# Chunk inverses of a recurrent mixer: block products of 64 for both heads in place of block-diagonal products of 128 for each

## The chip, the cores and the metric

One core of a Trainium2 chip runs the whole program. The metric is device time in microseconds of one execution; the time before is the median of three timed runs. TensorE (PE) multiplies matrices into PSUM, VectorE (DVE) and ScalarE (ACT) work on tiles in SBUF and PSUM, GpSimd (POOL) does a little, and SyncE (SP) issues nearly all loads.

## What is computed

The program is a small network of two blocks on 512 tokens of width 1024. In the first block's first layer two recurrent mixers stand side by side, and the change touches one of them, `rwkv7_group`. It has 8 heads of width 64. With the sequence cut into chunks, each chunk solves a triangular system and then passes a state on:

```python
A_ab = pair(a_dec, b_inv, strict)
A_ak = pair(a_dec, k_inv, strict)
rhs = jnp.concatenate([a_dec, jnp.einsum('bhnls,bhnsv->bhnlv', A_ak, v)], axis=-1)
sol = lax.linalg.triangular_solve(jnp.eye(L, dtype=F32) - A_ab, rhs,
                                  left_side=True, lower=True, unit_diagonal=True)
```

`pair` is a masked product of two chunks' rows. The mixers are followed by an output projection, cross-attention, a gated feed-forward, a second layer with other mixers, and a second block with retention, differential attention and a mixture of 32 experts. The outcome is one tensor of 512 x 1024.

## The kernel before

Every wide projection is done by `dense` (line 407): a weight tile is loaded into `raw` by SP, split into a high and a low part (`whi` by ACT at L383, `wlo` by DVE at L384), and 24 matmuls of 512 columns add up in a PSUM tile `acc`. All matmuls go through the helper `mm` (L348), so that the names of their operands tell them apart: `pp<-Q,XP` writes the PSUM tile `pp` from the tiles `Q` and `XP`.

The mixer works with chunks of 64 tokens. A tile of 128 x 512 holds four pairs of chunks: the pair's 128 tokens on the partitions and, side by side, four blocks of 128 columns. `rwkv_front` (the first half) makes the projections and the decayed vectors of two heads; `rwkv_back` (L773) makes the chunk inverses, the outputs and the state of two heads. There are four passes of two heads each. `merge` weaves a pass of `rwkv_back` with the next pass's `rwkv_front`, by the weights 45 and 27, or, in the fourth pass, with the keys and values of the memory (`mem_kv`). It calls in turn the part that is least far on for its weight, by the numbers that each `yield` gives. This sets priorities; the scheduler then fixes the order on each engine, and each engine runs its order strictly.

In `rwkv_back`, `pair(e, ...)` (L788) makes the products for head `e`: 64 rows of the array (that head's 64 components), 128 x 128 results, of which only the two diagonal blocks of 64 x 64 mean anything, as a chunk has nothing to do with its neighbour. `Am` holds A for one head. `X` and `P` are the inverse and its transpose, started as the identity with the first level copied in by a mask (L811 to L818). Then five levels double the size of the blocks that are solved (L843 on). At each level, for each head:

```python
pq = prod(Am[e], P[e])
TT(t4(Q[e]), t4(pq), b4(self.c("levt", l)), op=OP.mult)
...
pp = prod(X[e], Q[e])
if l < 5:
    px = prod(Q[e], X[e])
TT(P[e], pp, P[e], op=OP.add)
```

`prod` (L799) is four fp32 matmuls of 128 x 128 by 128 columns, one for each pair of chunks. So Q needs P; P and X need Q; the next level's Q needs P. The head-by-head order gives two such chains. `rest()` supplies the other products of the pass (`aak`, `Arb`, `Ark`, `pv`) between the levels. After the last level `prod(P[e], R[e])` gives Z (`pp<-R,XP`), and the state goes from chunk to chunk (`pT`, `pS`, `pw`, `py`).

Small tiles of 128 x 512 (`Am`, `Q`, `Z` and so on) come from a ring of 23 buffers, `self.f`; PSUM tiles of one bank each from a pool of five, `self.px`.

Three groups of small matmuls elsewhere in the trace are 64 x 64, each in one quadrant of the array (its rows are the partitions of the operands, its columns those of the result). `po<-qd,S` in `gla` alternates the halves `us` of the result, with the rows of one head, into one PSUM tile. `pkv<-vt,ket` in `gla` goes through both chunks of a pair (rows) and both heads (columns), with one PSUM tile for each chunk. `py<-reff,S` in `rwkv_back` has for head 0 the upper rows and the lower half of the result, for head 1 the opposite, with one PSUM tile for each head.

Of the kernel before, what the change touches and what calls it, by code (L numbers as in the profile page):

```python
# [11 lines left out]
I32 = mybir.dt.int32  # L12
AF = mybir.ActivationFunctionType
OP = mybir.AluOpType
# [168 lines left out]
def constants():  # L183
    A = {}
    i = np.arange(128)
    ident = np.eye(128, dtype=np.float32)
    c = i // 64
# [10 lines left out]
    for l in range(6):  # L198
# [3 lines left out]
        lev.append(off.astype(np.float32))  # L202
    A["cm"] = np.ascontiguousarray(np.concatenate(
        [ident, bones, bsw, m_incl, m_incl_sw, m_strict_sw, lev[0]] + [x.T for x in lev], axis=1))
    seg = np.ones((128, 512), np.float32)
    seg[:, ::64] = 0.0
    A["seg64"] = seg
# [74 lines left out]
class Net:  # L282
# [363 lines left out]
    def rwkv_lora(self):  # L646

        nc, A = self.nc, self.A
        self.vz = []
        for j in range(2):  # L650
            t = self.per.tile([128, 4, 192], F32, name=f"vz{j}")
            nc.gpsimd.memset(t[:, :, 64:128], 0.0)
            self.vz.append(t)
        self.wa2, self.wg2, self.lr, self.sgl = self.four("lora")
        self.yb = self.four("y")
        nc.sync.dma_start(self.wa2, A["rw_wa2"])
        nc.sync.dma_start(self.wg2, A["rw_g2"])
        lr = self.shift(self.dense(A["w_ab"], 8, 8, self.x), self.v("mu_lr1"), "lr", self.lr)
        nc.scalar.activation(lr[:64], lr[:64], AF.Tanh)
        yield 5  # L660
        sgl = self.shift(self.dense(A["w_ab"], 9, 8, self.x), self.v("mu_lr2"), "sgl", self.sgl)
        nc.scalar.activation(sgl, sgl, AF.Sigmoid)
        yield 5
# [109 lines left out]
    def rwkv_back(self, p, d, y):  # L773
# [6 lines left out]
        fs = slice(128 * p, 128 * p + 128)  # L780
        adec, binv, kinv, rdec, R, vt, ZV, BKt, sd, v = (
            d[n] for n in ("adec", "binv", "kinv", "rdec", "R", "vt", "ZV", "BKt", "sd", "v"))
        idb = b4(self.ident)
        rr = [slice(64 * e, 64 * e + 64) for e in range(2)]
        hc = [slice(64 - 64 * e, 128 - 64 * e) for e in range(2)]
        tiles = [slice(i * 128, i * 128 + 128) for i in range(4)]
# [9 lines left out]
            TT(t4(t), t4(ps), b4(self.c(mask)), op=OP.mult)  # L796
            return t

        def prod(x, z):  # L799
            ps = self.px("pp")  # L800
            for s in tiles:
                self.mm(ps[:, s], x[:, s], z[:, s])
            return ps


        Am, X, P = [], [], []
        inv = self.four("XP")
        pairs = self.four("Arb")
        for e in range(2):
            x, pt_ = inv[2 * e:2 * e + 2]  # L810
            nc.scalar.copy(t4(x), idb)  # L811
            nc.scalar.copy(t4(pt_), idb)
            ps = pair(e, adec, binv)
            am = self.f("Am")
            nc.scalar.copy(am, ps)
            nc.vector.copy_predicated(t4(x), b4(self.c("lev0").bitcast(I32)), t4(ps))
            ps = pair(e, binv, adec)
            nc.vector.copy_predicated(t4(pt_), b4(self.c("levt").bitcast(I32)), t4(ps))  # L818
            Am.append(am)
            X.append(x)  # L820
            P.append(pt_)
            yield 1.7
        Arb, Ark = [None, None], [None, None]

        def rest():
# [13 lines left out]

        rest = rest()  # L840
        for l in range(1, 6):
            Q = [None, None]
            for e in range(2):  # L843
                pq = prod(Am[e], P[e])
                Q[e] = self.f("Q")
                TT(t4(Q[e]), t4(pq), b4(self.c("levt", l)), op=OP.mult)
                yield 0.9
            for e in range(2):
                pp = prod(X[e], Q[e])
                if l < 5:  # L850
                    px = prod(Q[e], X[e])
                TT(P[e], pp, P[e], op=OP.add)
                if l < 5:
                    TT(X[e], px, X[e], op=OP.add)
                yield 1.7
                next(rest, None)
        for _ in rest:
            yield 0.9
        Z = []
        ZS = self.f("ZS")  # L860
        for e in range(2):
            pz = prod(P[e], R[e])
            z = self.f("Z")
            nc.scalar.copy(t4(ZS)[:, :, rr[e]], t4(pz)[:, :, rr[e]])
            nc.scalar.copy(z, pz)
            for c in range(2):
                nc.scalar.copy(ZV[rr[c], :, c, hc[e]], t4(pz)[rr[c], :, hc[e]])
            Z.append(z)
            yield 0.9
# [1470 lines left out]
def emit(ctx, tc, A, upto="all", dbg=None):  # L2340
    pctx, wctx = ExitStack(), ExitStack()
    N = Net(ctx, pctx, wctx, tc, A)
    ctx.push(pctx)
    ctx.push(wctx)
    nc = tc.nc

    def dump(name, tiles):
        for m, t in enumerate(tiles):
            nc.sync.dma_start(dbg[name][m], t)

    hb = N.four("h") + N.four("h")
    N.pre = []
    for m in range(8):
        N.resid(m, None, "g_mix0", True, hb[m])
        if m in (0, 3):
            N.pre.append(N.split_w2(A["w_gv"], 2 * len(N.pre)))
    nc.sync.dma_start(N.ident_, A["cm"][:, :128])
    y = [None] * 8
    d = [{} for _ in range(4)]

    def head():
        yield from N.rwkv_lora()
        N.memory()
        yield from N.rwkv_front(0, d[0])

    merge((N.gla(y), 95), (head(), 36))
    N.early()
    N.clear(N.zD, N.big("zero"))
    for p in range(4):
        back = (N.rwkv_back(p, d[p], y), 45)  # L2370
        if p < 3:
            merge(back, (N.rwkv_front(p + 1, d[p + 1]), 27))
        else:
            kv = [{}, {}]
            merge(back, (N.mem_kv(0, N.mem_operand(), kv[0]), 48))
    if upto == "rwkv":
        return dump("y", y)
    N.project(A["w_mo"][0], 8, N.operand(y), "g_xa0", first=True)
    if upto == "mix0":
        return dump("y", [N.hD[m] for m in range(8)])  # L2380
    N.xattn(0, kv[0])
    if upto == "xa0":
        return dump("y", [N.hD[m] for m in range(8)])
    ada = N.ada_parts()
    N.ffn(0, "g_mix1", ada[:6])
    if upto == "ffn0":
        return dump("y", [N.hD[m] for m in range(8)])
    y = [None] * 8
    d = [{} for _ in range(4)]

    def two(a):
        yield from N.mlstm_in(a, d[a])
        yield from N.mlstm_in(a + 1, d[a + 1])

    def first():
        yield from N.mlstm_gates()
        yield from two(0)

    merge((N.rglru(y), 51), (first(), 34))
    mo = N.mem_operand()  # L2400
    merge((N.mlstm_head(0, d[0], y), 7), (N.mlstm_head(1, d[1], y), 7), (two(2), 28))
    merge((N.mlstm_head(2, d[2], y), 7), (N.mlstm_head(3, d[3], y), 7), (N.mem_kv(1, mo, kv[1]), 48))
    if upto == "y1":
        return dump("y", y)
    N.project(A["w_mo"][1], 8, N.operand(y), "g_xa1")
    N.xattn(1, kv[1])
    N.ffn(1, None, ada[6:])
    N.norm_pair()
    M = Moe(ctx, N)
    ahead = [M.fetch for _ in range(BIG - 2)]  # L2410
    h2 = N.block2_mix(ahead)
    if upto == "h2":
        return dump("y", h2[0])
    wctx.close()
    N.route(*h2, ahead, M.early)
    pctx.close()
    M.open()
    M.run()
# [17 lines left out]
```

## Time and profile before

| what | value |
|---|---|
| median of three timed runs | 3314.12 us (3313.49 to 3316.09) |
| the profiled execution, its own time | 3308.96 us |
| its span, first instruction to last | 3307.1 us |
| PE busy, share of the span | 3216.8 us, 97% |
| PE weight loads (PEld) | 2564.3 us, 78% |
| DVE busy | 2347.8 us, 71% |
| ACT busy | 1832.9 us, 55% |
| mean granted TensorE clock | 0.987 |

A busy PE means that some matmul is under way; since matmuls are pipelined and overlap, it does not mean that the array is full. An fp32 matmul leaves two records of PE and two of PEld. The timeline merges neighbouring records of one kind: start, time from the first start to the last end, and their number. A row of the lines view gives the count, the busy time, the mean duration of one record, and after the second bar the idle time of the engine ahead of it, with what ended it. The four passes of `rwkv_back` run from 160.9 to 484 us.

### The profile page before, as it was taken

To read this page: it belongs to the slowest core of one execution; us is meant where nothing else is said; L and a number is where in the kernel's file an instruction comes from. 1 tells how busy PE (TensorE), PEld (TensorE's weight loads), DVE (VectorE), ACT (ScalarE), POOL (GpSimd) and SP (SyncE) were. 2 spreads that over 40 slices of the span, in tenths; PEclk is the share of its full clock that TensorE was granted. 3 is DMA by queue.
4 is the path that set the end of the run, shared out by engine and by line. 5 is a ranking of instruction groups with operands and counts; after the bars stand their busy time and mean duration, and the time that the engine had idled before them with its cause. 6 is when DMAs were issued, how large, how long until landed. Compare 5 with 4: busy or idle time off the path is not lost. (4 is left out here: it accounts for less than half of the span.)

```text
span 3307.1 us, 40569 instructions
## 1 busy us (share of the span) xinstructions
PE 3216.8 (97%) x15334; PEld 2564.3 (78%) x15335; DVE 2347.8 (71%) x3023; ACT 1832.9 (55%) x2356; POOL 205.4 (6%) x139
## 2 busy tenths in 40 slices
PE   8999999999999999999999998899999999999997
PEld 6688887777876787777877765688888888788885
DVE  5677765577634665577634354799999999999997
ACT  6643334443425864443434355577777777777774
POOL 1000001100000001100011000100110010111000
PEclk9999999999999999999999999899999999999999
DMA  5201123344333234345334312799999999999994
GB/s 167 79 20 29 43 89 121 122 168 169 90 125 111 75 118 126 126 147 184 90 110 135 128 50 105 275 355 360 366 366 366 353 358 367 359 358 357 369 358 161
DMA packets 152967, 649.61 MB, mean 196 GB/s; under 512 B 21335, under 2 KB 26543, under 8 KB 103228
## 3 DMA queue, kind: packets, MB, share of 16 engines
q1 hardware_dynamic: 143836, 630.86, 52.3%
q0 software_dynamic: 8928, 16.09, 1.9%
q8 instruction: 122, 2.00, 0.2%
q14 instruction: 81, 0.66, 0.1%
HBM read 626.55 MB, written 36.75 MB: 201 GB/s over the span
## 5 line engine op out<-in xcount | busy, mean ns | idle before, releaser
L1990 DVE TENSOR_TENSOR wlo<-w,whi 128x2048 fp32r<-128x2048 f32 x384 | 868.2, 2288 | 81.2 <-ACT whi L1989 76.5
L1989 ACT CAST whi<-w 128x2048 fp32r<-128x2048 f32 x384 | 729.7, 1908 | 295.9 <-PE hid L1981 178.5
L348 PE MATMUL acc<-x,whi 128*128 128x512 f32 (+1 forms) x2656 | 861.9, 404 | 7.2 <-ACT x L420 2.6
L383 ACT CAST whi<-raw 128x512 fp32r<-128x512 f32 (+1 forms) x578 | 352.8, 613 | 727.8 <-PE acc L348 600.6
L384 DVE TENSOR_TENSOR wlo<-raw,whi 128x512 fp32r<-128x512 f32 (+1 forms) x578 | 394.2, 685 | 389.8 <-ACT whi L383 373.5
L348 PEld LDWEIGHTS acc<-x,whi 128*128 128x128 f32 (+1 forms) x2656 | 496.1, 188 | 155.3 <-issue 25.4
L348 PE MATMUL acc<-x,wlo 128*128 128x512 f32 (+1 forms) x1328 | 534.0, 402 | 0.0
L1981 PE MATMUL hid<-whi,xh 128*128 128x512 f32 x1024 | 412.5, 403 | 4.5 <-DVE ln L2084 4.5
L1981 PE MATMUL hid<-whi,xl 128*128 128x512 f32 x1024 | 402.5, 393 | 2.6 <-DVE xl L1990 2.6
L348 PEld LDWEIGHTS acc<-x,wlo 128*128 128x128 f32 (+1 forms) x1328 | 250.0, 188 | 66.1 <-issue 6.3
L1981 PE MATMUL hid<-wlo,xh 128*128 128x512 f32 x1024 | 278.2, 393 | 0.0
L1981 PEld LDWEIGHTS hid<-whi,xh 128*128 128x128 f32 x1024 | 193.8, 189 | 46.2 <-issue 5.5
L1981 PEld LDWEIGHTS hid<-wlo,xh 128*128 128x128 f32 x1024 | 193.5, 189 | 42.7
L1981 PEld LDWEIGHTS hid<-whi,xl 128*128 128x128 f32 x1024 | 194.0, 189 | 41.7 <-DVE xl L1990 3.1
L1981 PE MATMUL y<-whi,ah 128*128 128x512 f32 x512 | 200.8, 392 | 0.7 <-ACT ah L1989 0.7
L1981 PE MATMUL y<-whi,al 128*128 128x512 f32 x512 | 200.3, 391 | 0.9 <-DVE al L1990 0.9
L348 PE MATMUL acc<-act,whi 128*128 128x512 f32 x512 | 162.6, 398 | 0.0
L1981 PE MATMUL y<-wlo,ah 128*128 128x512 f32 x512 | 158.8, 391 | 0.5 <-DVE wlo L1990 0.5
L455 POOL TENSOR_TENSOR sq<-sq,hs 128x512 f32<-128x512 f32 x42 | 56.2, 1339 | 1207.5 <-ACT hs L454 1207.1
L2121 POOL DMA_INDIRECT zD<-ys,sl x30 | 79.0, 2634 | 776.2 <-ACT sel L2043 466.5
L348 PEld LDWEIGHTS acc<-act,whi 128*128 128x128 f32 x512 | 95.2, 188 | 27.0 <-issue 5.1
L1981 PEld LDWEIGHTS y<-whi,ah 128*128 128x128 f32 x512 | 96.1, 188 | 22.6 <-ACT ah L1989 1.1
(651 smaller groups left out, 4653.7 us busy)
## 6 DMA issues: line engine op xcount, KB each, us to landing
w<-in_w_dram SPq DMA_DIRECT2D x384, 1024.0 KB, 8.2
raw<-in_w_up_dram SPq DMA_DIRECT2D x86, 512.0 KB, 3.5
wada<-in_w_ada_dram SPq DMA_DIRECT2D x96, 256.0 KB, 5.0
raw<-in_w_dn_dram SPq DMA_DIRECT2D x32, 512.0 KB, 3.6
h<-hD SPq DMA_DIRECT2D x48, 256.0 KB, 2.8
raw<-in_w_ab_dram SPq DMA_DIRECT2D x22, 512.0 KB, 3.6
hD<-hn SPq DMA_DIRECT2D x40, 256.0 KB, 2.0
raw<-in_w_k_dram SPq DMA_DIRECT2D x16, 512.0 KB, 3.5
```

The costliest lines, as they stand in the source:

```text
L348: self.nc.tensor.matmul(out, l, r, start=start, stop=stop)
L383: nc.scalar.copy(hi[:, :w], raw[:, c:c + w])
L384: nc.vector.tensor_tensor(lo[:, :w], raw[:, c:c + w], hi[:, :w].bitcast(F32), op=OP.subtract)
L455: nc.gpsimd.tensor_tensor(self.sq, self.sq, s, op=OP.add)
L1981: self.nc.tensor.matmul(out, l, r, start=start, stop=stop)
L1989: self.nc.scalar.copy(hi, src)
L1990: self.nc.vector.tensor_tensor(lo, src, hi.bitcast(F32), op=OP.subtract)
L2121: self.nc.gpsimd.indirect_dma_start(out=self.n.zD, out_offset=bass.IndirectOffsetOnAxis(ap=sl[:, 0:1], axis=0), in_=ys, in_offset=None, bo ...
```

## The change

A and the two matrices of the inverse are kept as their diagonal blocks alone: for each chunk a block of 64 x 64, the upper chunk of a pair on partitions 0 to 63, the lower one on 64 to 127. A head then takes 256 columns, and both heads fit in one tile of 128 x 512 (`X`, `P`, `Am`, `Q`). `pair_c` makes the blocks with 16 matmuls of 64 x 64 by 64 columns over the four quadrants of the array, into one PSUM tile for each head. `prod_c` makes one product of a level for both heads with 16 matmuls that alternate between the quadrant of the upper rows and columns and that of the lower ones, into one PSUM tile. The masks of 64 x 64 come as a new constant `cmc`, loaded once into a buffer of the ring. The products with R take 8 matmuls of 128 columns in the same two quadrants for each head. Heads no longer alternate within a level; `next(rest)` is called after Q too, and the weight of `rwkv_back` goes from 45 to 32. Nothing else is touched.

```diff
--- before.py
+++ after.py
@@ -202,6 +202,9 @@
         lev.append(off.astype(np.float32))
     A["cm"] = np.ascontiguousarray(np.concatenate(
         [ident, bones, bsw, m_incl, m_incl_sw, m_strict_sw, lev[0]] + [x.T for x in lev], axis=1))
+
+    A["cmc"] = np.ascontiguousarray(np.concatenate(
+        [np.concatenate([x[:64, :64], x[64:, 64:]]) for x in [ident, lev[0]] + [x.T for x in lev]], axis=1))
     seg = np.ones((128, 512), np.float32)
     seg[:, ::64] = 0.0
     A["seg64"] = seg
@@ -653,6 +656,8 @@
             self.vz.append(t)
         self.wa2, self.wg2, self.lr, self.sgl = self.four("lora")
         self.yb = self.four("y")
+        self.cmc = self.f("cmc")
+        nc.sync.dma_start(self.cmc, A["cmc"])
         nc.sync.dma_start(self.wa2, A["rw_wa2"])
         nc.sync.dma_start(self.wg2, A["rw_g2"])
         lr = self.shift(self.dense(A["w_ab"], 8, 8, self.x), self.v("mu_lr1"), "lr", self.lr)
@@ -780,7 +785,6 @@
         fs = slice(128 * p, 128 * p + 128)
         adec, binv, kinv, rdec, R, vt, ZV, BKt, sd, v = (
             d[n] for n in ("adec", "binv", "kinv", "rdec", "R", "vt", "ZV", "BKt", "sd", "v"))
-        idb = b4(self.ident)
         rr = [slice(64 * e, 64 * e + 64) for e in range(2)]
         hc = [slice(64 - 64 * e, 128 - 64 * e) for e in range(2)]
         tiles = [slice(i * 128, i * 128 + 128) for i in range(4)]
@@ -796,30 +800,44 @@
             TT(t4(t), t4(ps), b4(self.c(mask)), op=OP.mult)
             return t
 
-        def prod(x, z):
+
+
+        t8 = lambda t: t.rearrange("p (i l) -> p i l", l=64)
+        cm = lambda j, n: self.cmc[:, 64 * j:64 * j + 64].unsqueeze(1).to_broadcast([128, n, 64])
+        cols = [slice(j * 64, j * 64 + 64) for j in range(8)]
+        half = [slice(256 * e, 256 * e + 256) for e in range(2)]
+
+        def pair_c(x, z):
+            ps = [self.px("pA") for _ in range(2)]
+            for i in range(4):
+                for c in range(2):
+                    t = slice(128 * i + 64 * c, 128 * i + 64 * c + 64)
+                    for e in range(2):
+                        self.mm(ps[e][rr[c], cols[i]], x[rr[e], t], z[rr[e], t])
+            return [t[:, :256] for t in ps]
+
+        def prod_c(x, z):
             ps = self.px("pp")
-            for s in tiles:
-                self.mm(ps[:, s], x[:, s], z[:, s])
+            for s in cols:
+                for c in range(2):
+                    self.mm(ps[rr[c], s], x[rr[c], s], z[rr[c], s])
             return ps
 
-
-        Am, X, P = [], [], []
         inv = self.four("XP")
+        X, P = inv[:2]
         pairs = self.four("Arb")
+        Am = self.f("Am")
+        for t in (X, P):
+            nc.scalar.copy(t8(t), cm(0, 8))
+        ps = pair_c(adec, binv)
         for e in range(2):
-            x, pt_ = inv[2 * e:2 * e + 2]
-            nc.scalar.copy(t4(x), idb)
-            nc.scalar.copy(t4(pt_), idb)
-            ps = pair(e, adec, binv)
-            am = self.f("Am")
-            nc.scalar.copy(am, ps)
-            nc.vector.copy_predicated(t4(x), b4(self.c("lev0").bitcast(I32)), t4(ps))
-            ps = pair(e, binv, adec)
-            nc.vector.copy_predicated(t4(pt_), b4(self.c("levt").bitcast(I32)), t4(ps))
-            Am.append(am)
-            X.append(x)
-            P.append(pt_)
-            yield 1.7
+            nc.scalar.copy(Am[:, half[e]], ps[e])
+            nc.vector.copy_predicated(t8(X[:, half[e]]), cm(1, 4).bitcast(I32), t8(ps[e]))
+        yield 1.7
+        ps = pair_c(binv, adec)
+        for e in range(2):
+            nc.vector.copy_predicated(t8(P[:, half[e]]), cm(2, 4).bitcast(I32), t8(ps[e]))
+        yield 1.7
         Arb, Ark = [None, None], [None, None]
 
         def rest():
@@ -839,27 +857,28 @@
 
         rest = rest()
         for l in range(1, 6):
-            Q = [None, None]
-            for e in range(2):
-                pq = prod(Am[e], P[e])
-                Q[e] = self.f("Q")
-                TT(t4(Q[e]), t4(pq), b4(self.c("levt", l)), op=OP.mult)
-                yield 0.9
-            for e in range(2):
-                pp = prod(X[e], Q[e])
-                if l < 5:
-                    px = prod(Q[e], X[e])
-                TT(P[e], pp, P[e], op=OP.add)
-                if l < 5:
-                    TT(X[e], px, X[e], op=OP.add)
-                yield 1.7
-                next(rest, None)
+            pq = prod_c(Am, P)
+            Q = self.f("Q")
+            TT(t8(Q), t8(pq), cm(2 + l, 8), op=OP.mult)
+            yield 0.9
+            next(rest, None)
+            pp = prod_c(X, Q)
+            if l < 5:
+                px = prod_c(Q, X)
+            TT(P, pp, P, op=OP.add)
+            if l < 5:
+                TT(X, px, X, op=OP.add)
+            yield 1.7
+            next(rest, None)
         for _ in rest:
             yield 0.9
         Z = []
         ZS = self.f("ZS")
         for e in range(2):
-            pz = prod(P[e], R[e])
+            pz = self.px("pp")
+            for i, s in enumerate(tiles):
+                for c in range(2):
+                    self.mm(pz[rr[c], s], P[rr[c], cols[4 * e + i]], R[e][rr[c], s])
             z = self.f("Z")
             nc.scalar.copy(t4(ZS)[:, :, rr[e]], t4(pz)[:, :, rr[e]])
             nc.scalar.copy(z, pz)
@@ -2367,7 +2386,7 @@
     N.early()
     N.clear(N.zD, N.big("zero"))
     for p in range(4):
-        back = (N.rwkv_back(p, d[p], y), 45)
+        back = (N.rwkv_back(p, d[p], y), 32)
         if p < 3:
             merge(back, (N.rwkv_front(p + 1, d[p + 1]), 27))
         else:
```

TensorE's order, second pass, from the first level's P and X to the third level's Q, before (`pp<-XP,Am` is the product for Q, `pp<-Q,XP` that for P, `pp<-XP,Q` that for X; `pA` and `pv` are products of `rest()`, `pn` belongs to the next pass's front):

```order
L348 MATMUL pp<-Q,XP 128x128 x4
L348 MATMUL pp<-XP,Q 128x128 x4
L348 MATMUL pA<-adec,kinv 128x128 x4
L348 MATMUL pp<-Q,XP 128x128 x4
L348 MATMUL pp<-XP,Q 128x128 x4
L348 MATMUL pv<-vz_334,aak 128x128 x4
L348 MATMUL pp<-XP,Am 128x128 x8
L348 MATMUL pp<-Q,XP 128x128 x4
L348 MATMUL pp<-XP,Q 128x128 x4
L348 MATMUL pn<-k2s,cm 128x512
```

and in the change:

```order
L351 MATMUL pp<-Q,XP 64x64 x16
L351 MATMUL pp<-XP,Q 64x64 x16
L351 MATMUL pv<-vz_334,aak 128x128 x4
L351 MATMUL pp<-XP,Am 64x64 x16
L351 MATMUL pA<-adec,kinv 128x128 x4
L351 MATMUL pp<-Q,XP 64x64 x16
L351 MATMUL pp<-XP,Q 64x64 x16
L351 MATMUL pn<-k2s,cm 128x512
L351 MATMUL pv<-vz_334,aak 128x128 x4
L351 MATMUL pp<-XP,Am 64x64 x16
```

The products of both heads, four matmuls each and eight for the two Qs, have become one product of 16 small ones. Where the other head's product stood between a Q and its use, one `pA` of four matmuls stands now.

TensorE's order, third pass, from the last product of `rest()` to the end of the inverse, before (`acc` is a projection of the next front, `pT` the first step of the state):

```order
L348 MATMUL pA<-rdec,kinv 128x128 x4
L348 MATMUL pp<-XP,Am 128x128 x4
L348 MATMUL acc<-x,whi 128x512 x2
L348 MATMUL acc<-x,wlo 128x512
L348 MATMUL acc<-x,whi 128x512 x2
L348 MATMUL acc<-x,wlo 128x512
L348 MATMUL pp<-XP,Am 128x128 x4
L348 MATMUL pp<-Q,XP 128x128 x8
L348 MATMUL pp<-R,XP 128x128 x8
L348 MATMUL pT<-ZVBK,ZS 128x128 x7
```

and in the change:

```order
L351 MATMUL pA<-rdec,kinv 128x128 x4
L351 MATMUL pp<-XP,Am 64x64 x16
L351 MATMUL acc<-x,whi 128x512 x2
L351 MATMUL acc<-x,wlo 128x512
L351 MATMUL acc<-x,whi 128x512
L351 MATMUL pp<-Q,XP 64x64 x16
L740 MATMUL pt<-cm,adec 128x128 x4
L351 MATMUL acc<-x,whi 128x512
L351 MATMUL acc<-x,wlo 128x512
L351 MATMUL acc<-x,whi 128x512
L351 MATMUL pp<-R,XP 64x128 x8
L747 MATMUL pt<-cm,vsw 128x128 x4
```

Before, the last Q's products, those with R and `pT` followed each other directly; now projections (`acc`) and transposes (`pt`) stand between them.

## Rows read from the trace of the kernel before

**Rows 1.** Windows view, the four passes: length, PE, PEld, DVE, ACT, POOL busy, PEclk, DMA.
```profile
160.90:237.35 76.45, 76.16 (x542) 65.43 (x542) 53.74 (x97) 28.71 (x51) 0.00 (x0) 1.00 0.07 24
237.35:314.70 77.35, 76.70 (x544) 65.78 (x543) 54.26 (x97) 31.53 (x58) 0.00 (x0) 1.00 0.07 21
314.70:389.80 75.10, 71.17 (x534) 62.35 (x533) 55.66 (x101) 31.69 (x60) 0.00 (x0) 1.00 0.10 29
389.80:484.00 94.20, 93.94 (x703) 85.29 (x702) 63.52 (x104) 30.98 (x56) 0.00 (x0) 1.00 0.27 85
sum 323.10, PE 317.98 PEld 278.85 DVE 227.17 ACT 122.91 POOL 0.00; mean PE 79.49 PEld 69.71 DVE 56.79 ACT 30.73 POOL 0.00
```

**Rows 2.** Timeline, PE, 191 to 196 us: start, us, engine, line, instruction, operands, records.
```profile
191.12 1.05 PE L348 MATMUL pp<-Q,XP 128*128 128x128 f32 x8
192.01 1.06 PE L348 MATMUL pp<-XP,Q 128*128 128x128 f32 x8
193.00 1.16 PE L348 MATMUL pA<-rdec,binv 64*128 64x128 f32 x8
194.08 1.16 PE L348 MATMUL pp<-Q,XP 128*128 128x128 f32 x8
195.08 1.06 PE L348 MATMUL pp<-XP,Q 128*128 128x128 f32 x8
```

**Rows 3.** Waits view of SP's queue, 2060 to 3300 us: total, times, longest.
```profile
SPq L1935 <- DVE wlo L1990: 919.9, 339, 8.1
```

**Rows 4.** Tile view of pp and pA: the first x counts records; duration min/median/max.
```profile
L348 PE MATMUL pp<-XP,Am x320: 270/275/377, 165.4 to 450.7; 128*128 128x128 f32 x160
...
L348 PE MATMUL pp<-Q,XP x320: 270/275/377, 171.8 to 455.2; 128*128 128x128 f32 x160
...
L348 PE MATMUL pp<-XP,Q x256: 275/275/275, 172.7 to 444.8; 128*128 128x128 f32 x128
...
L348 PE MATMUL pp<-R,XP x64: 270/275/377, 215.2 to 459.8; 128*128 128x128 f32 x64
...
L348 PE MATMUL pA<-binv,adec x64: 269/272/373, 160.9 to 392.1; 64*128 64x128 f32 x64
```

**Rows 5.** Timeline, PE, two cuts from 228.05 us: one quadrant alone.
```profile
228.10 0.33 PE L348 MATMUL py<-reff,S 64*64 64x64 f32 x2
228.10 0.56 PE L348 MATMUL py<-reff,S 64*64 64x64 f32 x6
```

**Rows 6.** Timeline, PE, 92.3 to 94.1 us: two quadrants by turns (x4, x8).
```profile
92.74 0.33 PE L348 MATMUL po<-qd,S 64*64 64x64 f32 x4
93.00 0.49 PE L348 MATMUL po<-At,vt 128*128 128x128 f32 x2
93.42 0.45 PE L348 MATMUL po<-qd,S 64*64 64x64 f32 x8
93.80 0.49 PE L348 MATMUL po<-At,vt 128*128 128x128 f32 x2
```

**Rows 7.** Timeline, PE, 230.0 to 230.5 us: two quadrants on a diagonal.
```profile
230.11 0.33 PE L348 MATMUL py<-reff,S 64*64 64x64 f32 x4
```

**Rows 8.** Timeline, PE, two cuts from 88.5 us: four quadrants, 128 columns.
```profile
88.58 0.34 PE L348 MATMUL pkv<-vt,ket 64*64 64x128 f32 x4
88.58 1.09 PE L348 MATMUL pkv<-vt,ket 64*64 64x128 f32 x28
```

**Rows 9.** Lines view, 160.9 to 484 us: count, busy, mean ns, idle before and its releaser.
```profile
L846 DVE TENSOR_TENSOR Q<-pp,cm 128x512 f32<-128x512 f32 x40 | 27.3, 687 | 9.3 <-PE pp L348 9.3
```

**Rows 10.** Timeline, PE and DVE, at 449 and at 367 us: Q of the last level.
```profile
448.88 2.05 PE L348 MATMUL pp<-XP,Am 128*128 128x128 f32 x16
...
450.97 0.69 DVE L846 TENSOR_TENSOR Q<-pp,cm 128x512 f32<-128x512 f32 x1 [0.20 <-PE pp L348]
...
366.95 1.16 PE L348 MATMUL pp<-Q,XP 128*128 128x128 f32 x8 [2.34 <-DVE Q L846]
```

**Rows 11.** Waits view of PE, 160.9 to 484 us: total, times, longest.
```profile
PE pp L348 <- DVE Q L846: 2.3, 1, 2.3
```

## The prediction

> **What bounds the kernel now.** I cut the trace first into the four passes of the recurrent mixer, each from its first pA<-binv,adec matmul to the next one, with the windows view [rows 1]. TensorE is busy 317.98 of the 323.10 us, at a granted clock of 1.00 throughout; VectorE, the next engine, is busy 227.17 us. So TensorE sets the pace here, and what counts is how long its instructions occupy it. The span of one matmul does not tell that, since matmuls overlap; the step from one start to the next does. The timeline gives steps: eight records of 128 columns on the whole array take 0.89 us (191.12 to 192.01), 0.111 us each, and one fp32 matmul leaves two records [rows 2]. The rest of the program need not eat up a gain made here: later the weight queue waits on the engine's own side (919.9 us for VectorE to free a buffer), not for memory [rows 3], and every later stage starts from the end of this one. What the four passes lose in length, the kernel loses.
>
> **The products.** The three kinds of doubling products leave 320 + 320 + 256 = 896 records [rows 4], at 0.111 us 99.5 us of TensorE. The change computes only the diagonal blocks of 64, both heads in one tile: 14 products in a pass of 16 matmuls each, 896 matmuls in four passes, 1792 records. They alternate between the upper left and the lower right quadrant of the array. What does such a record cost? One quadrant alone: four more records lengthen the group from 0.33 to 0.56 us, 0.058 us each [rows 5]. Two quadrants by turns: four more lengthen it from 0.33 to 0.45 us, 0.030 us each [rows 6]; there (po<-qd,S) the two share the rows of the array and differ in its columns. Two quadrants on a diagonal (py<-reff,S) are in the trace too, four records in 0.33 us [rows 7], which is the 0.33 us that two records take in one quadrant [rows 5]. I take 0.030: 1792 x 0.030 = 53.8 us, a saving of **45.7 us**. The bounds: 0.0275 (0.11 us for the four, within the row's rounding) saves 50; 0.058 gives 104 us, a loss of 4.4 us (rival 2).
>
> **The pairs for A.** pA<-binv,adec and pA<-adec,binv leave 64 + 64 records of 128 columns [rows 4], 128 x 0.111 = 14.2 us. They become 128 matmuls of 64 columns, 256 records, over all four quadrants. The nearest row has four quadrants with 128 columns: 24 more records in 1.09 - 0.34 us, 0.031 each [rows 8]. For 64 columns the cost lies between half of that and all of it, 0.0155 to 0.031; [rows 2, 5] show that half the columns take half the step (0.111 to 0.058), so I take 0.0155: 4.0 us, a saving of **10.2 us** (6.3 at the other end).
>
> **The products with R** keep their length: 64 records of 128 columns on the whole array [rows 4] at 0.111 us against 128 in two quadrants by turns, at twice the 0.031 of [rows 8] 7.9 us: 0.8 us more at worst, taken as nothing.
>
> **The price: switching the array's shape.** When the shape of the tile changes, the step before and the first step after are longer. In [rows 2] the group with half the rows goes 1.08 us where 0.89 would do, the one before it 0.99 and the one after it 1.00: 0.10 + 0.19 + 0.10 = 0.39 us for two switches. In [rows 6] 0.80 us pass from 93.00 to 93.80 for two whole-array records (0.22) and eight quadrant records (0.24): 0.34 us for two, 0.17 each. I counted the switches in both orders of TensorE, over the four passes: 82 before, 170 in the change, since a product that stood between whole-array work without a switch is now an excursion. 88 x 0.17 = **15.0 us** lost (16.7 at 0.19).
>
> **VectorE and ScalarE.** Q and the two additions fall from 112 instructions of 0.69 us to 56, both heads in one [rows 9]: 38 us less on an engine that is not the bound, so nothing by itself. The masked copies are half as wide and the copies of A halve as well. The new constants cost one load of 256 KB on SP's queue, far ahead of their use; it delays the next weight tile, and TensorE has weight tiles in hand there: nothing. They also hold one of the 23 ring buffers, while A and Q take half the buffers they took: nothing.
>
> **The chain.** Before, two heads went through the levels as two chains, each covering the other's wait on VectorE. Now there is one chain, and what covers the wait has to be other work in TensorE's order. After a product's last record has ended, VectorE starts 0.04 us later (448.88 + 2.05 = 450.93, start 450.97) and takes 0.69 us [rows 10]: some 0.8 us until the next product may start. The change's order, shown above for the second pass, has something at each of these places. The usual short cover of a Q is four pA matmuls with half the rows of the array, 8 x 0.111 us and two switches, 1.2 to 1.3 us, at the last level three projections; the addition into P runs under the product that updates X (32 x 0.030 = 0.96 us), and further matmuls follow. So a step waits only where VectorE is late, and its load per us stays as it was: 227 of 323 before, about 185 of 280 now. TensorE idled 5.1 us in the four passes (323.10 - 317.98), 3.9 of it in the third, where the covering projections had run out: 2.34 us on a Q [rows 10]. In the change's order that place has three to four projection matmuls, so I take 2.3 us of the old idle time as gone and expect the rest to stay: **2.3 us** saved, between 5.1 saved and rival 1.
>
> **The sum.** 45.7 + 10.2 - 15.0 + 2.3 = 43.2 us saved. The profiled execution took 3308.96 us, which would make it 3265.8. The median of the three timed runs is 3314.12, 5.2 us above the profiled one, and I forecast against it: **3271 us**.
>
> **Rival 1: the single chain shows.** If at half of the 20 Q steps VectorE holds something back as in [rows 10], 2.34 us each, 23 us come back: 3294 us. For it: VectorE is busy 70% of the time and takes its instructions in order, and the row shows what a queue ahead of one Q costs. Against it: such covers stand at each step, and of the 40 such steps before, TensorE waited at one [rows 9, 11].
>
> **Rival 2: the two quadrants do not run together**, the one that ends slower. In [rows 6] the two quadrants have the same rows, and in [rows 7] the two on the diagonal write different banks, because each head has its own PSUM tile there. The new products combine both: different rows of the array, one bank. No row shows that pair. If it goes one after the other, each record costs 0.058, the products save nothing (-4.4 us), the products with R take 128 x 0.111 instead of 7.1 us (-7.1), and the pairs (one bank for each half of the rows) still save 10.2: -4.4 - 7.1 + 10.2 - 15.0 + 2.3 = 14 us slower, 3328 us. It decides from about 0.051 us a record on: there 1792 x 0.051 = 91 us and 5 us more for R use up what 99.5 + 10.2 - 15.0 + 2.3 = 97 us leave. For it: the missing row. Against it: the two write different partitions of the bank, and [rows 6] already has two quadrants writing different partitions of one bank at once. The Trainium skill ("TensorEngine Tiling (Array Packing)", Gotcha 1: PSUM Pressure) states that different row tiles cannot access the same PSUM bank simultaneously and that software must see to it. Taken to the letter that speaks against this change; taken as a stall it gives rival 2's 3328 us. The skill's "PSUM — Partial Sum Buffer" (PSUM bank collisions raise a hardware error) says of two TensorE writes that different column tiles may use one bank on disjoint partitions, which holds of these quadrants as well, and by it the forecast stands. No run here shows which of the two governs.
>
> **Rival 3: the change is made, but the time is not passed on**, because a later transfer ends last anyway: within 7 us of 3314; against it stands [rows 3], where SP's weight loads wait for the engines.
>
> **How the numbers follow.** Forecast 0.74, rival 1 0.13, rival 2 0.09, rival 3 0.04. About 0.2%, 6.6 us, is what a measurement of this kernel can tell from no change. Faster by more: forecast and rival 1, 0.87. Within it: rival 3, and the few cases in which two rivals meet, 0.04. Slower: 0.09. The range runs from the forecast with all the idle time gone (2.8 us more) and 0.0275 a record (4.5 us more), 3263 us, to rival 1, 3295 us. Rivals 2 and 3 stay outside.
>
> **What would show it.** Right: in the changed profile, sixteen quadrant records of pp go by in about 0.48 us, a product of 32 in some 0.96 us next to one of the same shape; the four passes together take about 280 us at a granted clock of 1.00; waits of TensorE for Q and XP stay near 5 us in all; from the end of the fourth pass on the two traces run in step. Wrong: pp records 0.058 us apart (rival 2); the windows of the passes shorter, but with 20 us and more of TensorE waiting for VectorE's Q or XP (rival 1); switches that cost far more than 0.17 us between quadrants and tiles with half the rows, a pair of shapes that has no row before.

## The result and the profile after

The changed kernel takes 3264.14 us (median of four runs, 3261.58 to 3265.99) against 3313.8 (3313.2 to 3316.09): ratio 0.9848, 95% interval 0.9831 to 0.9865. That is 49.7 us less, or 1.5%; 43.2 were forecast. The time lies within the forecast range of 3263 to 3295 us, 1 us above its lower end and 7 us under the 3271 us that were forecast. The profiled execution took 3265.32 us, with a span of 3263.1 us at a mean granted clock of 0.986.

The windows view of the changed kernel, cut at the same places as [rows 1] (first matmul of each pass to the next, the fourth to the end of its last pg; length, then busy time of PE, PEld, DVE, ACT, POOL, then granted clock and DMA):

```profile
160.08:222.25 62.17, 61.84 (x799) 48.58 (x799) 43.12 (x82) 27.02 (x50) 0.00 (x0) 1.00 0.06 21
222.25:286.76 64.51, 64.24 (x810) 50.67 (x810) 43.42 (x82) 28.11 (x53) 0.00 (x0) 1.00 0.08 26
286.76:351.08 64.32, 63.68 (x817) 51.39 (x816) 46.01 (x88) 30.40 (x59) 0.00 (x0) 1.00 0.13 42
351.08:433.30 82.22, 81.84 (x971) 71.00 (x971) 52.79 (x89) 30.14 (x55) 0.00 (x0) 1.00 0.28 91
sum 273.22, PE 271.61 PEld 221.64 DVE 185.33 ACT 115.67 POOL 0.00; mean PE 67.90 PEld 55.41 DVE 46.33 ACT 28.92 POOL 0.00
```

The four passes are 49.9 us shorter (323.10 to 273.22), at the same clock of 1.00. TensorE's idle time in them went from 5.1 to 1.6 us. A little of the 49.9 only moved: 12 pv matmuls with the weights (0.23 us each) now stand behind the last pg. So a mark further on is needed: the first VectorE instruction x<-hn,pv,x after the projection that follows the passes. In the timeline it starts here, in the kernel before, in the change, and in the change run again on another occasion:

```profile
617.73 0.75 DVE L424 SCALAR_TENSOR_TENSOR x<-hn,pv,x 128x512 fp32r<-128x512 f32 x1 [0.72 <-ACT x L423]
```
```profile
569.84 0.75 DVE L427 SCALAR_TENSOR_TENSOR x<-hn,pv,x 128x512 fp32r<-128x512 f32 x1 [0.71 <-ACT x L426]
```
```profile
573.58 0.75 DVE L427 SCALAR_TENSOR_TENSOR x<-hn,pv,x 128x512 fp32r<-128x512 f32 x1 [0.71 <-ACT x L426]
```

From the first matmul of the first pass (160.91, 160.08 and 163.81) these are 456.82, 409.76 and 409.77 us. This **stretch** agrees to a hundredth of a microsecond between the two executions of the change, far better than whole kernels do, and the change shortens it by 47.1 us. What lies behind it does not belong to the change: from the mark to the end of the span, 2689.4 us before, 2693.3 in the profiled execution of the change, 2689.6 in its repeat. All variants below are compared by this stretch as well as by their medians.

The timeline of TensorE in the second pass, which answers to [rows 2] (start, length to the last end, records):

```profile
253.46 1.15 PE L351 MATMUL pp<-Q,XP 64*64 64x64 f32 x32
254.44 1.10 PE L351 MATMUL pp<-XP,Q 64*64 64x64 f32 x32
255.47 1.16 PE L351 MATMUL pA<-rdec,kinv 64*128 64x128 f32 x8
256.55 1.15 PE L351 MATMUL pp<-XP,Am 64*64 64x64 f32 x32
```

A product of both heads, 32 records, takes 0.98 us from its start to the next (253.46 to 254.44), near the forecast's 0.96; two products of one kind took 16 records of 0.111 before. The half-row group pA between quadrant products takes 1.08 us (255.47 to 256.55), as it did between whole-array products [rows 2]: the new pair of shapes costs what the old one did.

The waits view of TensorE from 160 to 433 us, against [rows 11]: this is all of it.

```profile
PE pS L351 <- DVE Ts L897: 0.6, 1, 0.6
PE pp L351 <- DVE XP L839: 0.4, 1, 0.4
```

No wait for Q is left; before it was 2.3 us. Last, VectorE by lines in the four passes, against [rows 9]: twenty Q where there were forty, of the same length, and 15 us of VectorE's idle time are spent waiting for TensorE's product, so VectorE is early, not late.

```profile
L862 DVE TENSOR_TENSOR Q<-pp,cmc 128x512 f32<-128x512 f32 x20 | 13.8, 690 | 15.4 <-PE pp L351 15.3
```

### The profile page after: what moved, and what is told of

Same layout as the page of the kernel before. It is cut to its first block, busy times and chain, and to the rows that moved or that the text cites. A ratio compares the mean times of both kernels' runs of the same rounds, so it can differ in the third digit from the quotient of the medians.

```text
span 3263.1 us, 42667 instructions
## 1 busy us (share of the span) xinstructions
PE 3175.3 (97%) x16422; PEld 2509.1 (77%) x16423; DVE 2309.4 (71%) x2967; ACT 1826.8 (56%) x2348; POOL 205.0 (6%) x139
```

## Experiments

All are edits of the changed kernel. "Stretch" is the time defined above, read from one profile each.

| variant | median us (range) | ratio to the kernel before, 95% | stretch us | against the change |
|---|---|---|---|---|
| kernel before | 3313.8 | 1 | 456.8 | +47.1 |
| the change, run again | 3263.56 (3260.65 to 3267.68) | 0.985 [0.9835, 0.9865] | 409.8 | 0 |
| quadrants not by turns | 3303.13 (3301.7 to 3308.05) | 0.997 [0.9958, 0.9981] | 449.1 | +39.3 |
| old pairs for A | 3276.69 (3274.25 to 3281.14) | 0.9892 [0.9876, 0.9909] | 422.0 | +12.2 |
| weight 45 | 3274.3 (3267.96 to 3278.38) | 0.9885 [0.9868, 0.9901] | 417.0 | +7.2 |
| heads apart | 3272.94 (3271.18 to 3273.46) | 0.9876 [0.9861, 0.9891] | 416.7 | +6.9 |
| no placed cover | 3260.01 (3255.6 to 3263.7) | 0.9843 [0.983, 0.9857] | 404.8 | -5.0 |
| masked pairs by halves | 3250.93 (3249.32 to 3254.62) | 0.9816 [0.9802, 0.983] | 397.6 | -12.1 |
| masked pairs by quadrants | 3247.64 (3246.75 to 3252.32) | 0.9808 [0.9794, 0.9822] | 393.0 | -16.8 |
| ... and pv by quadrants | 3249.0 (3244.76 to 3252.13) | 0.9806 [0.9793, 0.9819] | 393.2 | -16.6 |
| ... and no placed cover | 3248.84 (3247.53 to 3251.49) | 0.9807 [0.9793, 0.982] | 394.5 | -15.3 |

**The disputed prices by themselves.** After the passes the kernel gets groups of matmuls on constant tiles, between whole-array groups W of sixteen records.

```
+ A:  for s in cols: for c in range(2): mm(a[rr[c], s], x[rr[c], s], z[rr[c], s])
+ B:  the same, c = 0 into tile a, c = 1 into tile b (two banks)
+ C:  as A, with c as the outer loop
+ D:  as A, with x[rr[0], s], z[rr[0], s]   (same rows of the array)
+ E:  for s in cols[:4]: for c: for e: mm((a, b)[e][rr[c], s], x[rr[e], s], z[rr[e], s])
+ F:  for s in tiles: for e: mm((a, b)[e][:, s], x[rr[e], s], z[rr[e], s])
+ G:  four times: one whole-array matmul, two of A    H: the same with a half-row matmul
```

> Groups of matmuls on constant data are added after the four passes, between whole-array groups of eight records, twice over; the output stays that of the kernel. Theory (two diagonal quadrants in one bank run together, and the bank plays no part): A, by turns in one bank, 32 records in 0.94 to 1.0 us; B, the same in two banks, the same within 0.03 us; C, one quadrant after the other, 1.8 to 1.9 us; D, two quadrants with the same rows, as A; E, four quadrants in two banks, 0.48 to 0.6 us; F, upper and lower half-row tiles by turns in two banks, 16 records of 128 columns, 0.9 us if halves of rows run together and 1.78 us if not; G and H, eight switches between a quadrant pair and whole-array or half-row tiles, 2.7 us each at 0.17 us a switch. Rival (one bank costs something when rows differ): B faster than A by over 0.1 us.

The timeline of TensorE there, first round (the start of the next row ends each group):

```profile
444.25 1.15 PE L351 MATMUL bA<-bz,bx 64*64 64x64 f32 x32
445.33 2.05 PE L351 MATMUL bW<-bz,bx 128*128 128x128 f32 x16
447.31 1.15 PE L351 MATMUL bB<-bz,bx 64*64 64x64 f32 x32
...
450.37 1.90 PE L351 MATMUL bC<-bz,bx 64*64 64x64 f32 x32
452.19 2.05 PE L351 MATMUL bW<-bz,bx 128*128 128x128 f32 x16
454.18 1.15 PE L351 MATMUL bD<-bz,bx 64*64 64x64 f32 x32
...
457.24 0.69 PE L351 MATMUL bE<-bz,bx 64*64 64x64 f32 x32
457.86 2.05 PE L351 MATMUL bW<-bz,bx 128*128 128x128 f32 x16
459.84 1.16 PE L351 MATMUL bF<-bz,bx 64*128 64x128 f32 x16
460.94 2.05 PE L351 MATMUL bW<-bz,bx 128*128 128x128 f32 x16
462.82 2.69 PE L351 MATMUL bG<-bz,bx 128*128 128x128 f32 x24
465.44 2.05 PE L351 MATMUL bW<-bz,bx 128*128 128x128 f32 x16
467.42 2.78 PE L351 MATMUL bH<-bz,bx 64*128 64x128 f32 x24
470.13 2.05 PE L351 MATMUL bW<-bz,bx 128*128 128x128 f32 x16
```

A, B and D take 1.08 us each: for two quadrants that write different partitions the bank plays no part, nor does it matter whether they share the rows of the array (D) or not (A). Quadrants or halves that write the same partitions (E, F) were put into two banks; no run here has them in one. The 1.08 holds its share of the switches on both sides (about 0.05 us on entering, 0.09 on leaving), so 32 records take 0.94 us, 0.029 each (a pair starts every 0.058 us). C takes 1.82. E takes 0.62, 0.015 a record without its switches, the low end that the pairs' term was taken at. F, 16 records of 128 columns by halves of the rows, takes 1.10 where whole-array records would take 1.78: halves of the rows run together as well. G: 2.62 us, less four whole-array matmuls (4 x 0.223) and sixteen quadrant records (0.47), plus 0.10 by which the next W's first step is longer, leave 1.36 us for eight switches, **0.17 each**. H has nine (one more on entering, 0.09 us of it in the W ahead): 2.71 - 1.36 + 0.19 = 1.54, again 0.17. The rival (one bank costs something) falls.

**The turns undone.**

```
-            for s in cols:
-                for c in range(2):
+            for c in range(2):
+                for s in cols:
```

> Each product issues all eight matmuls of the upper left quadrant, then all eight of the lower right, instead of by turns; same matmuls, same result. Theory (two quadrants run together only while their records alternate in the order): sixteen records of one quadrant at 0.058 us, twice, so a product of 32 records takes about 1.85 us in place of 0.98; 56 products give 0.87 x 56 = 49 us, and the kernel takes 3310 to 3316 us, about what the kernel before took. Rival (the array takes work for a free quadrant from further back in the order, so the turns don't matter): 3262 to 3268 us and 0.98 us a product.

The timeline of the second pass in this variant:

```profile
253.36 0.27 PE L351 MATMUL pp<-XP,Q 64*64 64x64 f32 x1
253.41 0.22 PE L351 MATMUL pp<-Q,XP 64*64 64x64 f32 x1
253.47 0.22 PE L351 MATMUL pp<-XP,Q 64*64 64x64 f32 x1
253.47 0.22 PE L351 MATMUL pp<-Q,XP 64*64 64x64 f32 x1
253.53 0.22 PE L351 MATMUL pp<-XP,Q 64*64 64x64 f32 x1
253.53 0.22 PE L351 MATMUL pp<-Q,XP 64*64 64x64 f32 x1
253.59 1.67 PE L351 MATMUL pp<-XP,Q 64*64 64x64 f32 x29
...
257.13 1.90 PE L351 MATMUL pp<-XP,Am 64*64 64x64 f32 x32
258.96 0.50 PE L351 MATMUL acc<-x,whi 128*128 128x512 f32 x1
```

A product that stands alone takes 1.83 us (257.13 to 258.96), 0.75 us more than group A. 56 x 0.75 = 42 us; measured 39.3 in the stretch. Where two products follow each other, the second, in the upper quadrant, starts at 253.36, ahead of the last three records of the first, in the lower one (253.41, 253.47 and 253.53). So TensorE does not run its order quite strictly: it reaches past records that wait for a busy quadrant, but only three far, at each of the 16 places where two products meet. The same happens inside a product, where the upper quadrant's records end and the lower one's begin, in group C as well.

So the theory holds: the turns bring 39 of the 47 us. Its size was too large, 49 us, and the 3303.1 us lie below its range. Within a quadrant a record does take the 0.058 us of [rows 5], in group C too; what the theory lacked is the three records at each border, 3 x 0.058 = 0.17 us. The second quadrant's 16 records take 0.93 us; 56 x (0.93 - 0.17) = 42.6 us, less 16 x 0.17 between products, leave 39.8.

**The pairs for A undone.**

```
-        ps = pair_c(adec, binv)
-        for e in range(2):
-            nc.scalar.copy(Am[:, half[e]], ps[e])
...
+        for e in range(2):
+            ps = pair(e, adec, binv)
+            for c in range(2):
+                nc.scalar.copy(t8(Am[rr[c], half[e]]), blk(ps, c))
...
```

> Only the pairs for A are undone: eight matmuls of 64 rows by 128 columns for each kind and pass, from which the diagonal blocks are copied out in twice as many, half as wide copies; the products stay on quadrants. Theory (the pairs' term of the sum, 128 records at 0.111 against 256 at 0.0155 to 0.02): 9 to 10 us longer, 3272 to 3276 us. Rival (the pairs had been in the shadow of something else, as the waits between the two halves of pA suggest): under 4 us longer, 3264 to 3268 us.

12.2 us longer in the stretch, 13 by the medians, 0.7 us past the theory's range. The waits view of TensorE over the four passes (159 to 446 us):

```profile
PE pA L351 <- DVE XP L837: 2.0, 2, 1.1
...
```

With three smaller rows (0.8, 0.7 and 0.5) these are 4.0 us of waits in place of 1.0, which leaves 9.2 us for the pairs' own records, next to 10.2 forecast. Of the other 3 us, 2.1 are waits for VectorE's masked copies, which are twice as many here (2.0 and 0.5 us on XP in place of 0.4); the cause of the row of 0.8, on y at the end of the mixer, stays open.

**The weight of the merge.**

```
-        back = (N.rwkv_back(p, d[p], y), 32)
+        back = (N.rwkv_back(p, d[p], y), 45)
```

> The share of the mixer's back part in the merge goes back from 32 to 45 steps, so that it gets through its levels with less of the next front part's work between them. Theory (the short covers, pairs and projections, are enough for a chain of 0.8 us): the waits of TensorE for Q and XP stay under 6 us in all and the kernel takes 3262 to 3270 us. Rival (the smaller share is what hides the single chain): waits of 15 us and more in the four passes, 3278 us and over.

7.2 us longer in the stretch; the median, 3274.3, lies between the theory's range and the rival's. The rival's reason does not hold: TensorE waits for no Q. All of the 7.2 us is idle time (9.6 us in the stretch against 2.4); TensorE's busy time stays the same, 407.3 against 407.4 us, since the lower clock of one pass and 24 fewer changes of shape about cancel. The windows view shows one pass, the third, and its clock:

```profile
290.73:356.47 65.74, 58.10 (x773) 46.33 (x773) 43.30 (x82) 26.43 (x51) 0.00 (x0) 0.95 0.10 34
```

There TensorE idles 7.6 us and the granted clock falls to 0.95. The timeline at the end of that pass shows the steps of the mixer's tail with nothing between them, and the second of two like instructions, after the idle times, at about half the pace; the granted clock from 350 to 354 us is 0.50, the lower of its two levels (1.2 GHz):

```profile
347.18 1.12 PE L351 MATMUL pm<-yl,cm 128*128 128x512 f32 x2 [1.43 <-DVE yl L934]
349.89 2.07 PE L351 MATMUL pm<-y,cm 128*128 128x512 f32 x2 [1.58 <-ACT y L941]
```

What is missing is projections, as the lines view of the third pass tells, first in this variant, then in the change:

```profile
L351 PE MATMUL acc<-x,whi 128*128 128x512 f32 x22 | 7.3, 405 | 0.0
L351 PE MATMUL acc<-x,wlo 128*128 128x512 f32 x12 | 5.0, 413 | 0.0
```
```profile
L351 PE MATMUL acc<-x,whi 128*128 128x512 f32 x37 | 12.9, 414 | 0.0
L351 PE MATMUL acc<-x,wlo 128*128 128x512 f32 x19 | 7.6, 401 | 0.0
L351 PE MATMUL acc<-mp,whi 128*128 128x256 f32 x15 | 3.0, 289 | 0.0
L351 PE MATMUL acc<-mp,wlo 128*128 128x256 f32 x6 | 2.2, 363 | 0.0
```

34 against 77. With weight 45 the two earlier passes have 153 such records of `x` in place of 131, 22 of the 43 that are missing here; the other 21, those of the memory (`mp`), come only in the fourth pass. The kernel before had most of its idle time in the third pass too [rows 1]. The weight 32 matches the shorter levels; without it 7 us of the gain would be lost.

**The heads taken apart again.**

```
+            for e in range(2):
+                pq = prod_h(e, Am, P)
+                TT(t8(Q[:, half[e]]), t8(pq), cm(2 + l, 4), op=OP.mult)
...
```

> The two heads are taken apart again: each product has the 8 matmuls of one head (still two quadrants by turns), and VectorE has two half-width instructions for one of full width, in the order of steps of the kernel before. The order of TensorE has 193 switches of shape in the four passes in place of 170. Theory (joining the heads saves switches and nothing else, since neither one chain nor two is waited for): 23 x 0.17 = 4 us longer, 3265 to 3271 us. Rival (the joined tile matters for VectorE, which gets 56 instructions more): waits for Q and XP of 6 us and more, 3273 us and over. Rival (two chains cover each other better than one): under 3262 us.

6.9 us longer in the stretch, 3272.9 us: past the theory's range, at the edge of the first rival's. 23 switches are 3.9 us. The waits view of TensorE (158 to 450 us) gives 4.6 us in place of 1.0, 3.6 more; the sum, 7.5, is near the 6.9. Only 1.8 us of the 4.6 are waits for Q and XP, far from the 6 that the rival asked for; the others are on `adec` (1.2), `ZS` (1.1) and `rt` (0.5), and the last two stand in the next run as well, which has the heads joined.

```profile
PE pp L351 <- DVE Q L871: 1.6, 1, 1.6
...
PE pp L351 <- DVE XP L877: 0.2, 1, 0.2
```

One chain with both heads is therefore no weakness against two: with two there is a wait for Q, with one there is none.

**The placed cover taken away.**

```
             yield 0.9
-            next(rest, None)
             pp = prod_c(X, Q)
```

> The work that stands between a Q product and the two products that need Q (the step of the masked pairs and of pv) is issued after them instead, so that only what the merge puts there covers the single chain. In the order of TensorE the four passes then have 143 switches of shape in place of 170, 27 x 0.17 = 4.6 us less. Theory (the chain of 0.8 us from one product to the next is real, and this placement hides it): waits of TensorE for Q and XP of 6 to 14 us in all instead of 1, net 3265 to 3274 us. Rival 1 of the prediction in full (2.3 us at a step without cover): waits of 25 us and more, 3285 us and over. Rival (the cover was never needed): waits under 2 us, 3258 to 3262 us.

5.0 us shorter in the stretch. The switches explain it (27 x 0.17 = 4.6), and the waits view from 160 to 433 us has no row for Q at all. The timeline, VectorE and TensorE, shows what covers a Q now:

```profile
251.34 1.15 PE L351 MATMUL pp<-XP,Am 64*64 64x64 f32 x32
252.42 0.73 PE L351 MATMUL acc<-x,whi 128*128 128x512 f32 x2
252.53 0.69 DVE L862 TENSOR_TENSOR Q<-pp,cmc 128x512 f32<-128x512 f32 x1 [0.76 <-PE pp L351]
...
254.24 1.15 PE L351 MATMUL pp<-Q,XP 64*64 64x64 f32 x32
```

Projections of the merge fill the time from 252.42 to 254.24, and Q is ready at 253.22. Projections stand at all twenty such places of this run. Theory and first rival fall; "the cover was never needed" holds.

**The masked pairs by halves and by quadrants**, built on what groups E and F showed.

```
+            for s in tiles:                                  # by halves
+                for e in range(2):
+                    self.mm(ps[e][:, s], x[rr[e], s], z[rr[e], s])
+            for i in range(4):                               # by quadrants
+                for c in range(2):
+                    for e in range(2):
+                        self.mm(ps[e][rr[c ^ sw], t], x[rr[e], f], z[rr[e], t])
```

> The masked pairs aak, Arb and Ark of the two heads are issued together, one matmul of the upper and one of the lower half of the rows by turns, in two banks: 16 records of 128 columns in one group instead of two groups of 8. Theory (halves of the rows run together, 1.09 us for 16 records in the measured group against 2 x 0.89): 10 us less for 12 double groups and 25 fewer switches, 4.3 us, so 3248 to 3253 us. Rival (with 5 pieces to put between the products instead of 8, the chain shows at 20 or more steps by 0.5 us): 3258 us and over.

> The same pairs cut to their diagonal blocks, 16 matmuls of 64 columns over all four quadrants by turns for both heads; the blocks off the diagonal are set to zero by GpSimd, and each mask becomes two half-width instructions on VectorE. Theory (quadrants of four run at 0.0157 us a record, and beside a product there is no switch): 24 pairs of 0.89 us become 12 of 0.5 us, 15 us less, and 29 fewer switches, 5 us: 3242 to 3248 us. Rival (0.5 us is too short a cover for a chain of 0.8 us, and the zeros hold up VectorE): waits of TensorE for Q and XP of 10 us and more, 3254 us and over.

In the stretch 12.1 us less where the terms give 14.3, and 16.8 where they give 20; the medians, 3250.9 and 3247.6, lie inside what both theories expected. TensorE waits 2.2 us in all by halves and 3.7 by quadrants, in place of 1.0, so that part of the missing 2 to 3 us is the chain, which now shows a little. By quadrants its largest row is this one:

```profile
PE pp L351 <- DVE Q L882: 1.7, 5, 0.4
```

Two further steps brought nothing. With pv by quadrants:

> The variant with the masked pairs on four quadrants, and pv too is computed from the diagonal blocks of aak on two quadrants by turns, so that aak needs no zeros. Against that variant 6 fewer switches, 1.0 us less, and pv 16 records at 0.0625 us in place of 8 at 0.111, 8 x 0.11 = 0.9 us more. Theory: within 3 us of that variant, 3244 to 3250 us. Rival (the zeros on GpSimd were in the way): 3242 us or less.

393.2 against 393.0 us: the theory holds, the zeros were not in the way. With the pieces behind the products of the level as well:

> As the run before, but the pieces (pairs and pv) stand behind the products of each level instead of between Q and its two products. The order has 134 switches of shape against 137. Theory (the merge's own work covers the chain, as in the run without the cover): waits for Q under 2 us, 3242 to 3248 us. Rival (with the pieces on quadrants there is too little other work between Q and its products): waits of 5 us and more for Q, 3250 us and over.

394.5 us, and the waits view now has this row:

```profile
PE pp L351 <- DVE Q L885: 6.0, 11, 1.8
```

The longest of these waits, in the third pass, shows in the timeline:

```profile
312.18 1.72 DVE L860 TENSOR_TENSOR Arb<-pA,cm 64x256 f32<-64x256 f32 x4
313.93 0.69 DVE L885 TENSOR_TENSOR Q<-pp,cmc 128x512 f32<-128x512 f32 x1
314.67 0.79 PE L351 MATMUL pp<-Q,XP 64*64 64x64 f32 x18 [1.75 <-DVE Q L885]
```

The product for Q has ended at 312.92, but VectorE is still at the four half-width masks of the piece that now stands ahead of it, and starts Q 1 us late. These masks stand right ahead of Q at eight of the places with a wait. Where projections follow the product they cover most of such a delay (0.15 to 0.7 us are left); at two places in the third pass there are none, and these two waits (1.4 and 1.8 us) are half of the 6.0. The loss is small, 1.3 us, and its rival's time is not reached. The quickest variant, masked pairs by quadrants, is 16 us under the change; between the medians of the last three no difference can be told.

## Why the prediction was right, and where its sizes were off

**The mechanism.** Two diagonal quadrants in one bank run together, at 0.029 us a record; undoing the turns gives 39 us back. This was the step without a row in the trace of before, and rival 2 stood on it. That the time lies inside the range is in part luck: the products and the idle time alone, at their best, were its lower end, 3263 us, with no room for the spread between executions, and single executions of the change (3260.65 to 3267.68 us) fall on both sides of it.

**One bank for two quadrants.** The Trainium skill ("TensorEngine Tiling (Array Packing)", Gotcha 1: PSUM Pressure) states that different row tiles cannot access one PSUM bank simultaneously. Groups A and B contradict this for quadrants that write different partitions: 1.08 us with one bank, 1.08 with two. The Trainium skill's page "PSUM — Partial Sum Buffer" (PSUM bank collisions raise a hardware error) states that different column tiles may share a bank on disjoint partitions; groups A and D agree. The same section repeats the rule on row tiles, which the prediction passed over: the two pages do not differ, and here the measurement decides.

**The terms of the sum**, as the prediction put them, and what the runs showed:

| term | forecast us | measured us | from |
|---|---|---|---|
| products | +45.7 | 99.5 - 1792 x 0.0292 = +47.2 | group A without its switches |
| pairs for A | +10.2 | +9.2 to +10.3 | old pairs without their extra waits; group E |
| switches, 88 | -15.0 | 88 x 0.17 = -15.0 | groups G and H; 88 more changes of shape in the trace |
| idle time | +2.3 | 5.1 - 1.6 = +3.5 | windows |
| sum | 43.2 | 44.9 to 46.0 | stretch: 47.1 |

So the sum was 4 us short: 1.5 of it on the products (0.0292 in place of 0.030), 1.2 on the idle time, and one to two microseconds that no term explains. Of the 49.7 us by the medians a further 2.6 lie outside the stretch; runs of one kernel differ by more than that, and no cause was sought.

**VectorE's 38 us, "nothing by itself".** Right for its load as such, but the joined heads are worth some 7 us in all: about half of it switches, half waits of TensorE that stood in no term, of which 1.8 us on Q and XP.

**The chain (rival 1).** It did not show, as forecast, but the reason given was not the right one. The prediction named the four pA matmuls placed after each Q as the usual cover; without them nothing waits either, and the kernel is 5 us quicker. What covers a Q is the merge's projections, which in the change itself stand at 16 of the 20 places; pA stands alone at four, and there too it is long enough (1.0 us for a Q that takes 0.7). Where pA was a group of its own, the placed cover cost two switches. The merge's weight, which the prediction did not price at all, is worth 7 us, not by covering Q but by leaving projections for the third pass.

**Rivals 2 and 3** fall: a quadrant's records do run together, and the time is passed on. Both traces run in step behind the passes, 47.9 us apart at the projection and, in the repeat, the same 2690 us to the end.

## What to carry over

Small matmuls on two or four quadrants of the array run at two or four times the pace of one, and those on two halves of the rows at twice that of one half, if they stand by turns in the order; grouped by quadrant, most of that is lost. Two quadrants that write different partitions may share a bank at no cost in time; for those that write the same partitions, only separate banks were measured. Each change of shape costs 0.17 us, so work of one shape belongs side by side, and a small piece that is put between two products as a cover should first be shown to be needed. After shortening one partner of a merge, set its share anew: the partner's work otherwise runs out where it is needed.

## What was not expected of the hardware

The array starts records of a free quadrant past those that wait for a busy one, though only three records ahead (the rows from 253.36 on in the run without turns). Halves of the rows run together into two banks as quadrants do (group F: 1.10 us in place of 1.78). And a stage of 410 us that TensorE bounds came out alike to 0.01 us in two executions, while the remaining 2690 us vary by 4 us from one execution of the same kernel to the next.
